# A new order for a two-layer hybrid encoder: differential pairs moved ahead, eps adds and scan copies on other engines, and a table that shifts the planner's priorities

## The chip, the cores and the metric

The kernel runs on one core of one Trainium2 chip. The metric is the device time of one execution in microseconds (us): before the change 1492.83 us, the median of three runs (1492.78 to 1493.38).

## The reference

Two layers on 512 tokens of width 1024, all in float32. Each layer projects the residual stream once into three groups of heads, joins their outputs in one output projection with a LayerNorm behind it, and then runs a gated MLP with a small convolution and another LayerNorm. Cut to what matters:

```python
proj = x @ w_in                                  # 1024 -> 4608
da_q, da_k, da_v, hg_q, hg_ff, hg_fb, hg_i, hg_g, mx_q = split(proj)
# differential attention, 4 heads: two softmaxes over 512 keys each
p = softmax(s); a = p[:, :, 0] - lam * p[:, :, 1]; da_o = rms_norm(a @ v)
# HGRN2: a gated linear recurrence, forward and backward, 4 heads with a 128x128 state
hg_o = rms_norm(scan(q, k, v, g) + flip(scan(flipped))) * silu(hg_g)
# cross-attention into 256 memory rows, 4 heads
mx_o = softmax(mx_q @ mk.T) @ mv
x = layer_norm(alpha * x + concat(da_o, hg_o, mx_o) @ w_out)
u = depthwise_conv(x @ w_up); gate, val = split(u)
x = layer_norm(alpha * x + (silu(gate) * val) @ w_down)
```

## The kernel before

**Numbers.** Every large product is done with float16 matmuls: weights and activations are each split into a high and a low part (`wh`, `wl`; `xh`, `xl`; `mgh`, `mgl`), and three products of the parts are summed in PSUM (`mm3`, L314; all large matmuls are issued by the helper at L140). A weight is prepared in these steps (`prep`, L295 to L312): SP loads it (`wst`), ScalarE squares it and sums (L307), a tiny matmul with ones adds the sums up over the partitions (`stat`, L168), VectorE makes a power of two from it (L155, L157, L159), ScalarE writes the scaled high part (L310) and VectorE the low part (L311). Activations are split in the same way by `split_group` (L531): ScalarE squares each half (L536), VectorE adds the halves' sums where there are two halves (L540), a tiny matmul and three small steps give the scale, and VectorE writes the high part (L545) and the low part (L547).

**The work.** The heads go in pairs: two pairs each of HGRN2 ("hg"), memory attention ("mx") and differential attention ("da"). A pair has projection steps on TensorE and a *unit*, which is a generator of small pieces of work. In an hg unit the scan runs over five small block lengths (1 to 16) and then larger ones; per length, VectorE masks the block of scores (L851) and multiplies decays into queries and keys (L881, L885), and at length 16 GpSimd copies the diagonal blocks (L854). In a da unit VectorE takes maxima (L1039, L1040), ScalarE the exponentials (L1042), VectorE combines the two softmaxes (L1049 to L1051), and TensorE transposes the result (L513). In an mx unit VectorE takes the maxima (L952), ScalarE the exponentials (L957), VectorE divides (L962, L964), TensorE transposes (L968), and the result is copied out (L975). The root of the mean square is in `rms` (L516), the LayerNorm in `norm` (L223) and `layernorm` (L274): statistics and first product on VectorE (L227, L229, L280), epsilon and the power -0.5 on GpSimd (L231, L232), the second product on VectorE (L281), transposes on TensorE (L288), and the split into `xh` and `xl` (L292, L293).

The output projection (`down_part`, L554) goes token tile by token tile: TensorE fills one PSUM bank (`mm`), and VectorE drains it into the residual tile `z` (L569). The next product into that bank waits for the drain. The pieces of the output projection are: hg pair 0, hg pair 1, da pair 0 (each of them a `down`), then four tiles of mx (`out_mx`), and at the end the rest of mx with da pair 1, with LayerNorm 1 token tile by token tile (`out_last`, L1104 ff.).

**What sets the order.** `SEQ` (L43) lists in which order pairs, the rotary set-up and output pieces are put beside each other; `emit` (L596) walks through it and lets the units' pieces run beside projection and output steps. That gives the program one order of writing. `extract` (L1285) then reads the program's instructions with their dependences, `deadlines` (L1573) gives each one a due time, counted back from its consumers with planned costs, and `simulate` (L1417) lists the work of every engine and the choice of buffers by these due times. The resulting order per engine is imposed on the program; each engine then works in this order and waits where an operand or a buffer isn't ready.

Of the kernel before, what the change touches and what calls it, by code (L numbers as in the profile page):

```python
# [15 lines left out]
AF = mybir.ActivationFunctionType  # L16
ALU = mybir.AluOpType
AX = mybir.AxisListType

P = 128  # L20
S = 512
D = 1024
# [19 lines left out]
START = "c0123wv"  # L42
_seq = [("hg", 0), ("rope",), ("hg", 1), ("mx", 0), ("mx", 1), ("da", 0), ("out", "hg", 0), ("da", 1), ("out", "hg", 1), ("out", "da", 0)]  # L43
SEQ = [_seq, _seq]
# [51 lines left out]
def trunk(ctx: ExitStack, tc: tile.TileContext, a, out, slots=None):  # L96
# [126 lines left out]
    def norm(t, idx):  # L223
        zt = z[t]
        st = small(12, "bnst")
        for j in range(2):
            V.bn_stats(st[:, j * 6 : (j + 1) * 6], zt[:, j * 512 : (j + 1) * 512])  # L227
        mv = small(2, "bnmv")
        V.bn_aggr(mv, st)  # L229
        rs = small(1, "lnrs")  # L230
        G.tensor_scalar(rs, mv[:, 1:2], LN_EPS / (ALPHA * ALPHA if idx else 1.0), None, ALU.add)  # L231
        G.tensor_tensor(rs, rs, mhalf[:, 0:1], ALU.pow)  # L232
        return mv[:, 0:1], rs
# [282 lines left out]
    def rms(o, eps=None):  # L516
        sq = tmp([P, 4, P], "w2", bufs=4)
        A.activation(sq, o.rearrange("p (c v) -> p c v", c=4), AF.Square)
        ss = small(4, "rmss")
        V.tensor_reduce(ss, sq, AX.X, ALU.add)  # L520
        rs = small(4, "rmrs")
        if eps is None:
            G.tensor_scalar(rs, ss, 1.0 / P, RMS_EPS, ALU.mult, ALU.add)
        else:
            G.tensor_tensor(rs, ss, eps, ALU.add)
        G.tensor_tensor(rs, rs, mhalf, ALU.pow)
        on = tmp([P, 4, P], "w2", bufs=4)
        V.tensor_tensor(on, o.rearrange("p (c v) -> p c v", c=4), rs.unsqueeze(2).broadcast_to([P, 4, P]), ALU.mult)
        return transposes(on)
# [162 lines left out]
    def build_layer(l):  # L692
# [55 lines left out]
        def hg_units(pr):  # L748
# [57 lines left out]
            def hg_attn():  # L806
# [31 lines left out]
                while m < S:  # L838
                    nb = S // m
                    for j in range(2):  # L840
                        Q, K, At, Dg, Tm = Qs[j], Ks[j], As[j], Ds[j], Ts[j]
                        p_ = psc()
                        if m <= 16:
# [8 lines left out]
                            if m == 16:  # L852
                                for b in range(4):
                                    G.tensor_copy(diag_block(At, 32 * b, 32 * b, 32), Dg[32 * b : 32 * b + 32])  # L854
                        elif m <= 64:
# [368 lines left out]
class Op:  # L1224
    __slots__ = ("i", "name", "eng", "cost", "tail", "reads", "writes", "table", "preds", "succs", "tiles", "dmab", "line", "kind", "small", "order_ins", "mv", "istr", "half", "mode")

# [58 lines left out]
def extract(instrs):  # L1285
    ops = []
    last_half = None
    for i in instrs:
# [28 lines left out]
        o.writes = [b for b in outs if type(b.tensor).__name__ == "Tile"]  # L1317
        o.preds, o.succs = set(), []
        o.small = _n(outs[0].ap) <= 16 if outs else False
# [44 lines left out]
    for o in ops:  # L1364
        o.tiles = []
        for wr, bs in ((False, o.reads), (True, o.writes)):
            for b in bs:
# [9 lines left out]
                for (j, w2, a0, a1, m2) in h:  # L1377
                    if (wr or w2) and j != o.i:
                        if psum or (a0 < p1 and p0 < a1 and m & m2):
                            o.preds.add(j)  # L1380
        for wr, bs in ((False, o.reads), (True, o.writes)):
            for b in bs:
# [3 lines left out]
                if wr:  # L1386
                    if psum:
                        h[:] = []
                    else:
                        h[:] = [e for e in h if not (p0 <= e[2] and e[3] <= p1 and (e[4] & ~m) == 0 and e[0] != o.i)]  # L1390
                h.append((o.i, wr, p0, p1, m))
    for o in [o for o in ops if o.dmab][:FIRST]:
        o.dmab *= FAST
# [23 lines left out]
def simulate(ops, tiles, prio, fixed=None, wait=0.0, log=None):  # L1417
# [8 lines left out]
    mode = 128  # L1426
    dma_free = 0.0

# [55 lines left out]
    while done < N:  # L1484
# [60 lines left out]
        for s in o.succs:  # L1545
            lat = LAT if ops[s].eng != o.eng else (0.03 if e != "PE" else -o.tail)
            if ops[s].eng == "POOL" and e != "POOL":
# [16 lines left out]


PEN = 20.0
SHARE = 0.35
# [5 lines left out]
def deadlines(ops, tiles):  # L1573
# [32 lines left out]
    for k, o in enumerate([o for o in ops if o.dmab][:FIRST]):  # L1606
        D[o.i] = k - 1000.0
    return [T[o.i] if o.eng == "PE" else D[o.i] for o in ops]

# [50 lines left out]
```

## Time and profile before

| what | value |
|---|---|
| runs | 1493.38, 1492.83, 1492.78 us; median 1492.83 |
| profiled execution | 1492.88 us, of which the span of the trace is 1491.1 us |
| TensorE (PE) busy | 1451.7 us, 97% |
| VectorE (DVE) busy | 1168.4 us, 78% |
| ScalarE (ACT) busy | 865.1 us, 58% |
| GpSimd (POOL) busy | 130.1 us, 9% |

How to read the profile: L12 is line 12 of the kernel before. A row of a view names engine, line, operation, and what it writes from what it reads, in the program's names without buffer numbers. "Busy" leaves out the issuing of DMAs and the work on semaphores. Matmuls are pipelined, so one that is drawn 0.38 us long may have its successor start after about 0.22. A time in brackets is the idle time of the engine just before a row, with the instruction that ended it. PEclk is the clock that TensorE was granted, as a share of full speed. In time, the span holds: the start to 21 us, projections and scans of layer 0 to about 300, output projection to about 430 with LayerNorm 1, the MLP to 800, scans of layer 1 to 960, its softmax groups and output projection to 1150, its MLP to 1482, and the tail.

### The profile page before, as it was taken

The page shows a single profiled execution, that of the slowest core. Times are in us where ns is not written, and L with a number is a line of the kernel's source. Part 1 is how long each engine was busy: PE and PEld are TensorE (multiplying, and loading weights), DVE is VectorE, ACT ScalarE, POOL GpSimd, SP SyncE. Part 2 cuts the span into 40 slices and gives each one's busy share as a digit, 9 for nine tenths or more (in the row PEclk, how much of TensorE's full clock was granted, in tenths as well). Part 3 has the DMA queues.
Part 4 walks back from the last instruction along what each step waited for, and adds up shares of the span by engine and source line. Part 5 has one row for each costly group of instructions (what it writes and reads, how often), then busy time and mean ns, then how long its engine had stood idle before and what let it go on. Part 6 is the DMA issues. An engine that isn't in the chain of part 4 may idle for free. (4 is left out here: it accounts for less than half of the span.)

```text
span 1491.1 us, 24496 instructions
## 1 busy us (share of the span) xinstructions
PE 1451.7 (97%) x9978; PEld 811.9 (54%) x9978; DVE 1168.4 (78%) x2242; ACT 865.1 (58%) x1094; POOL 130.1 (9%) x154
## 2 busy tenths in 40 slices
PE   6999999999999999999999999999999999999997
PEld 4566675565564444444487475655656544444443
DVE  7989968978997677666785978789888777566777
ACT  5876655666376556455466656566645656455550
POOL 1001020000111101001000101001001101001011
PEclk9999999999999999999999999999999999999999
DMA  6342111223143323232324202112232323333221
GB/s 238 114 150 86 59 58 59 101 71 101 46 143 114 107 85 113 85 113 96 128 90 140 87 30 86 57 57 77 79 100 85 113 88 118 99 92 114 86 84 57
DMA packets 158171, 141.91 MB, mean 95 GB/s; under 512 B 3302, under 2 KB 139114, under 8 KB 158058
## 3 DMA queue, kind: packets, MB, share of 16 engines
q1 hardware_dynamic: 158058, 140.35, 29.2%
q8 instruction: 78, 1.28, 0.3%
q14 instruction: 35, 0.29, 0.1%
HBM read 138.24 MB, written 2.10 MB: 94 GB/s over the span
## 5 line engine op out<-in xcount | busy, mean ns | idle before, releaser
L140 PEld LDWEIGHTS <-wh 128*128 128x128 f16 x2624 | 251.0, 98 | 237.5 <-issue 3.4
L311 DVE SCALAR_TENSOR_TENSOR wl<-wst,ws,wh 128x2048 f16<-128x2048 f32 x122 | 312.5, 2561 | 52.3 <-ACT wh L310 51.4
L140 PE MATMUL mm<-xh,wl 128*128 128x512 f16 (+1 forms) x832 | 305.3, 367 | 0.6 <-DVE wl L311 0.6
L140 PE MATMUL mm<-xh,wh 128*128 128x512 f16 (+1 forms) x832 | 305.2, 367 | 0.0
L140 PE MATMUL mm<-xl,wh 128*128 128x512 f16 (+1 forms) x832 | 305.0, 367 | 0.0
L307 ACT ACTIVATE wh<-wst 128x2048 bf16<-128x2048 f32 x122 | 232.2, 1903 | 102.4 <-PE stat L168 49.2
L310 ACT ACTIVATE wh<-wst,ws 128x2048 f16<-128x2048 f32 x122 | 243.5, 1996 | 40.1 <-DVE ws L157 19.5
L140 PE MATMUL mm<-wh,t 128*128 128x512 f16 (+1 forms) x768 | 223.5, 370 | 0.0
L140 PEld LDWEIGHTS <-wl 128*128 128x128 f16 x1312 | 128.2, 98 | 123.0 <-DVE wl L311 0.9
L140 PEld LDWEIGHTS <-t 128*128 128x128 f16 x1152 | 110.2, 98 | 121.4 <-issue 0.6
L569 DVE SCALAR_TENSOR_TENSOR z<-mm,inv,z 128x512 f32<-128x512 f32 x176 | 130.2, 745 | 45.9 <-PE mm L140 32.2
L140 PE MATMUL sc<-xl,wh 128*128 128x512 f16 (+1 forms) x416 | 147.5, 355 | 0.0
L140 PE MATMUL sc<-xh,wl 128*128 128x512 f16 (+1 forms) x416 | 147.5, 355 | 0.0
L140 PE MATMUL sc<-xh,wh 128*128 128x512 f16 (+1 forms) x416 | 147.5, 355 | 0.0
L140 PE MATMUL mm<-wl,t 128*128 128x512 f16 (+1 forms) x384 | 142.1, 370 | 0.0
L155 DVE TENSOR_SCALAR we<-stat 128x1 int32<-128x1 int32 x122 | 18.6, 153 | 118.8 <-PE stat L168 118.6
L1151 POOL TENSOR_TENSOR t<-f 128x512 f32<-128x512 f32 x44 | 60.6, 1378 | 542.7 <-DVE f L1149 438.6
L140 PE MATMUL mm<-wh,mgh 128*128 128x512 f16 x192 | 73.3, 382 | 4.7 <-DVE z L569 4.7
L1147 ACT ACTIVATE f<-sc,cvb,cw 128x512 f32<-128x512 f32 x44 | 34.1, 775 | 71.4 <-PE stat L168 69.3
L140 PE MATMUL mm<-wh,mgl 128*128 128x512 f16 x192 | 72.9, 381 | 0.9 <-DVE mgl L547 0.6
L140 PE MATMUL mm<-wl,mgh 128*128 128x512 f16 x192 | 73.3, 382 | 0.0
L1042 ACT ACTIVATE f<-sc,dam,iqk 128x512 f32<-128x512 f32 x64 | 49.3, 774 | 38.8 <-DVE dam L1040 34.3
(244 smaller groups left out, 2125.4 us busy)
## 6 DMA issues: line engine op xcount, KB each, us to landing
wst<-in_w_up_dram SPq DMA_DIRECT2D x88, 512.0 KB, 4.3
wst<-in_w_in_dram SPq DMA_DIRECT2D x36, 1024.0 KB, 4.8
wst<-in_w_down_dram SPq DMA_DIRECT2D x22, 1024.0 KB, 4.9
wst<-in_w_out_dram SPq DMA_DIRECT2D x12, 1024.0 KB, 4.9
wst<-in_w_mem_kv_dram SPq DMA_DIRECT2D x8, 1024.0 KB, 5.0
z<-in_x_dram SPq DMA_DIRECT2D x4, 512.0 KB, 4.9
mix<-in_ln_g_dram SPq DMA_DIRECT2D x4, 512.0 KB, 3.6
mix<-in_ln_b_dram SPq DMA_DIRECT2D x4, 512.0 KB, 4.7
```

Of the source, the lines that this page charges most:

```text
L140: T.matmul(o, lhsT, rhs, start=start, stop=stop)
L155: V.tensor_scalar(e, tot.bitcast(I32), 0x7F000000, 1, ALU.bitwise_and, ALU.logical_shift_right)
L307: A.activation(h.rearrange("p a b -> p (a b)").bitcast(BF16), flat, AF.Square, accum_out=ss)
L310: A.activation(h.rearrange("p a b -> p (a b)"), flat, AF.Identity, scale=s)
L311: V.scalar_tensor_tensor(l.rearrange("p a b -> p (a b)"), flat, s, h.rearrange("p a b -> p (a b)"), ALU.mult, ALU.subtract)
L569: V.scalar_tensor_tensor(zs, p_, ivs[half % len(ivs)], zs, ALU.mult, ALU.add)
L1042: A.activation(pe[:, c, :], sc_[c], AF.Exp, bias=mx[:, c : c + 1], scale=iqk, accum_out=z1 if c else z0)
L1147: A.activation(c, p_, AF.Identity, scale=cw[:, 1, v : v + 1], bias=cvb[:, l, i + 22 * v : i + 22 * v + 1])
L1151: G.tensor_tensor(gt[:, n, :], c2[:, 0, :], c2[:, 1, :], ALU.mult)
```

## The change

1. `SEQ` is rewritten: the da pairs come right behind the hg pairs and the mx pairs behind them; of the output pieces, hg pair 0, hg pair 1 and da pair 0 now stand at the end. (Before, the mx pairs came first, and the output pieces stood between and behind the da pairs.)
2. The epsilon adds of `norm` and `rms` (L231, L523, L525) go from GpSimd to VectorE; the power -0.5 stays on GpSimd.
3. The copies of the diagonal blocks at length 16 (L854, 32 of 32x128) go from GpSimd to ScalarE.
4. The planner: an order between two reads of the same PSUM bank by one engine is kept in its planning as "soft" with a latency of its own, the first DMA is planned 2.1 us later, and a table `NUDGE` of some 280 rows (engine, from, to, shift) adds shifts to the due times of ranges of instructions.

```diff
-_seq = [("hg", 0), ("rope",), ("hg", 1), ("mx", 0), ("mx", 1), ("da", 0), ("out", "hg", 0), ("da", 1), ("out", "hg", 1), ("out", "da", 0)]
+_seq = [("hg", 0), ("rope",), ("hg", 1), ("da", 0), ("da", 1), ("mx", 0), ("mx", 1), ("out", "hg", 0), ("out", "hg", 1), ("out", "da", 0)]
...
-        G.tensor_scalar(rs, mv[:, 1:2], LN_EPS / (ALPHA * ALPHA if idx else 1.0), None, ALU.add)
+        V.tensor_scalar(rs, mv[:, 1:2], LN_EPS / (ALPHA * ALPHA if idx else 1.0), None, ALU.add)
...
-            G.tensor_scalar(rs, ss, 1.0 / P, RMS_EPS, ALU.mult, ALU.add)
+            V.tensor_scalar(rs, ss, 1.0 / P, RMS_EPS, ALU.mult, ALU.add)
         else:
-            G.tensor_tensor(rs, ss, eps, ALU.add)
+            V.tensor_tensor(rs, ss, eps, ALU.add)
...
-                                    G.tensor_copy(diag_block(At, 32 * b, 32 * b, 32), Dg[32 * b : 32 * b + 32])
+                                    A.activation(diag_block(At, 32 * b, 32 * b, 32), Dg[32 * b : 32 * b + 32], AF.Identity)
...
+                    elif psum and j != o.i and ops[j].eng == o.eng:
+                        o.soft.add(j)
...
+    for o in ops:
+        o.soft -= o.preds
+        o.preds |= o.soft
...
-    dma_free = 0.0
+    dma_free = 2.1
...
-            lat = LAT if ops[s].eng != o.eng else (0.03 if e != "PE" else -o.tail)
+            lat = LAT if ops[s].eng != o.eng else (0.03 if e != "PE" and i not in ops[s].soft else -o.tail)
...
+    (0, 2171, 2215, -9.43), (2, 8523, 8601, 7.46), (1, 3505, 3534, -45.27), (2, 8524, 8545, 0.73), (1, 7, 17, -1.14), (1, 9160, 9161, 8.8),
...
-    return [T[o.i] if o.eng == "PE" else D[o.i] for o in ops]
+    D = [T[o.i] if o.eng == "PE" else D[o.i] for o in ops]
+    for e, a, b, d in NUDGE:
+        for o in ops[a:b]:
+            if o.eng == ("PE", "DVE", "ACT", "POOL", "SP")[e]:
+                D[o.i] += d
+    return D
```

The first place is the queue of VectorE inside the softmax run of the differential pairs in layer 0, before the change (`f4` are softmax tiles, `dam` maxima, `daz1` sums, `z0` to `z3` the residual token tiles, `mm` a PSUM bank of the output projection):

```order
L569 SCALAR_TENSOR_TENSOR z1_78<-mm_740_4152,inv_726_4092,z1_78 128x512
L1049 RECIPROCAL daz1_679_3884<-daz1_679_3884 128x1
L1050 SCALAR_TENSOR_TENSOR daz1_679_3884<-daz1_679_3884,nlam0_328,daz_673_3867 128x1
L1039 TENSOR_REDUCE dam_687_3911<-sc_689_3913 128x1
L1039 TENSOR_REDUCE dam_687_3911<-sc_690_3914 128x1
L1051 SCALAR_TENSOR_TENSOR f4_681_3886<-f4_681_3886,daz1_679_3884 128x512
L1040 TENSOR_SCALAR dam_687_3911<-dam_687_3911,iqk_661_3796 128x2
L569 SCALAR_TENSOR_TENSOR z2_79<-mm_747_4185,inv_726_4092,z2_79 128x512
L311 SCALAR_TENSOR_TENSOR wl_725_4089<-wst_719_4077,ws_723_4085,wh_720_4079 128x2048
L569 SCALAR_TENSOR_TENSOR z3_80<-mm_749_4202,inv_726_4092,z3_80 128x512
```

The same kind of work in VectorE's queue after the change:

```order
L1040 TENSOR_SCALAR dam_578_3427<-dam_578_3427,iqk_559_3338 128x2
L1051 SCALAR_TENSOR_TENSOR f4_574_3412<-f4_574_3412,daz1_572_3410 128x512
L311 SCALAR_TENSOR_TENSOR wl_623_3631<-wst_617_3619,ws_621_3627,wh_618_3621 128x2048
L1049 RECIPROCAL daz1_577_3426<-daz1_577_3426 128x1
L1050 SCALAR_TENSOR_TENSOR daz1_577_3426<-daz1_577_3426,nlam0_328,daz_571_3409 128x1
L1039 TENSOR_REDUCE dam_585_3453<-sc_587_3455 128x1
L1039 TENSOR_REDUCE dam_585_3453<-sc_588_3456 128x1
L1051 SCALAR_TENSOR_TENSOR f4_579_3428<-f4_579_3428,daz1_577_3426 128x512
```

The drains (L569) that stood between the softmax steps are gone from this run; weights (L311) stand there as before. Between the first and the last L1051 of a layer there were 23 and 22 drains, and now there are 3 and 0. In the runs of the mx units (L952 to L975) there were none, and now there are 21 and 14.

The second place is the split of the mx halves in layer 1, on VectorE. Before, around the sum of the halves (`gss1`):

```order
L1040 TENSOR_SCALAR dam_1818_10627<-dam_1818_10627,iqk_1778_10411 128x2
L569 SCALAR_TENSOR_TENSOR z3_80<-mm_1879_10891,inv_1837_10692,z3_80 128x512
L540 TENSOR_REDUCE gss1_1757_10312<-gss_1754_10307 128x1
L157 TENSOR_SCALAR ws_1884_10907<-we_1883_10905 128x1
L159 TENSOR_SCALAR wi_1885_10909<-we_1883_10905 128x1
L326 TENSOR_SCALAR inv_1916_11082<-wi_1885_10909,lnin_82 128x1
L155 TENSOR_SCALAR ge_1759_10316<-tr_1758_10314 128x1
L157 TENSOR_SCALAR gs_1760_10318<-ge_1759_10316 128x1
L159 TENSOR_SCALAR gi_1761_10320<-ge_1759_10316 128x1
L545 TENSOR_SCALAR mgh_1755_10308<-mix_1676_9961,gs_1760_10318 128x1024
```

After the change (`mm_2025` is the bank of the last output product of da pair 0):

```order
L569 SCALAR_TENSOR_TENSOR z3_80<-mm_2025_11626,inv_2017_11568,z3_80 128x512
L326 TENSOR_SCALAR inv_2062_11761<-wi_2031_11644,gi_1903_11084 128x1
L540 TENSOR_REDUCE gss1_1984_11432<-gss_1981_11427 128x1
L155 TENSOR_SCALAR ge_1986_11436<-tr_1985_11434 128x1
L157 TENSOR_SCALAR gs_1987_11438<-ge_1986_11436 128x1
L159 TENSOR_SCALAR gi_1988_11440<-ge_1986_11436 128x1
L545 TENSOR_SCALAR mgh_1982_11428<-mix_1916_11136,gs_1987_11438 128x1024
L326 TENSOR_SCALAR inv_2040_11665<-wi_1999_11482,gi_1988_11440 128x1
L547 SCALAR_TENSOR_TENSOR mgl_1989_11443<-mix_1916_11136,gs_1987_11438,mgh_1982_11428 128x1024
```

And TensorE's rows at that place after the change:

```order
L140 MATMUL mm_2025_11626<-wl_1949_11279,mgh_1786_10511 128x512
L140 LDWEIGHTS mgl_1791_10522
L140 MATMUL mm_2025_11626<-wh_1944_11269,mgl_1791_10522 128x512
L168 LDWEIGHTS ones_74
L168 MATMUL tr_1985_11434<-gss1_1984_11432,ones_74 128x1
L140 LDWEIGHTS mgh_1982_11428
L140 MATMUL mm_2042_11669<-wh_1995_11474,mgh_1982_11428 128x512
```

The split moved from the middle of the softmax work to the last moment: its sum stands behind the drain of the product that TensorE finishes just ahead of the split's own tiny matmul. In layer 0 the order is the same.

The third place is VectorE at LayerNorm 1 of layer 1, before the change (`z1_78` and `z2_79` are the second and third token tile):

```order
L229 BN_AGGR bnmv_2073_11824<-bnst_2072_11821 128x2
L192 TENSOR_SCALAR lnbd_2058_11750<-lnbd_2058_11750 128x1
L280 SCALAR_TENSOR_TENSOR z1_78<-z1_78,bnmv_2073_11824,mix_2054_11742 128x512
L155 TENSOR_SCALAR lne_2059_11753<-lnbd_2058_11750 128x1
L280 SCALAR_TENSOR_TENSOR z1_78<-z1_78,bnmv_2073_11824,mix_2054_11742 128x512
L157 TENSOR_SCALAR lns_2060_11755<-lne_2059_11753 128x1
L281 SCALAR_TENSOR_TENSOR z1_78<-z1_78,lnrs_2074_11826,mix_2056_11746 128x512
L194 COPY lnsc_81<-lns_2060_11755 128x1
L281 SCALAR_TENSOR_TENSOR z1_78<-z1_78,lnrs_2074_11826,mix_2056_11746 128x512
L569 SCALAR_TENSOR_TENSOR z2_79<-mm_2077_11847,inv_2040_11665,z2_79 128x512
```

And after it:

```order
L229 BN_AGGR bnmv_2066_11782<-bnst_2065_11779 128x2
L227 BN_STATS bnst_2072_11821<-z1_78 128x6
L231 TENSOR_SCALAR lnrs_2067_11784<-bnmv_2066_11782 128x1
L280 SCALAR_TENSOR_TENSOR z0_77<-z0_77,bnmv_2066_11782,mix_2054_11742 128x512 x2
L281 SCALAR_TENSOR_TENSOR z0_77<-z0_77,lnrs_2067_11784,mix_2056_11746 128x512 x2
L569 SCALAR_TENSOR_TENSOR z2_79<-mm_2077_11847,inv_2040_11665,z2_79 128x512
L229 BN_AGGR bnmv_2073_11824<-bnst_2072_11821 128x2
L231 TENSOR_SCALAR lnrs_2074_11826<-bnmv_2073_11824 128x1
```

The same drain (from `mm_2077`) stood behind the second tile's whole normalization and now stands ahead of it, and the epsilon add (L231) is among VectorE's rows.

More of the change, by code (lines that the diff above doesn't have):

```diff
@@ L1224 @@
 class Op:
-    __slots__ = ("i", "name", "eng", "cost", "tail", "reads", "writes", "table", "preds", "succs", "tiles", "dmab", "line", "kind", "small", "order_ins", "mv", "istr", "half", "mode")
+    __slots__ = ("i", "name", "eng", "cost", "tail", "reads", "writes", "table", "preds", "succs", "tiles", "dmab", "line", "kind", "small", "order_ins", "mv", "istr", "half", "mode", "soft")
 def cost_of(i, kind, eng, outs, ins):
@@ L1317, in extract @@
         o.writes = [b for b in outs if type(b.tensor).__name__ == "Tile"]
-        o.preds, o.succs = set(), []
+        o.preds, o.succs, o.soft = set(), [], set()
         o.small = _n(outs[0].ap) <= 16 if outs else False
@@ L1563, in simulate @@
     return max(end), start, end, order, slot_of
+NUDGE = (
[44 rows of a table added]
+)
 PEN = 20.0
```

43 rows, old and new, of the table NUDGE are left out of this document.

## The prediction

> **What bounds the kernel now.** I read the page's busy shares first, then the table of stretches, then the waits of TensorE stretch by stretch, then the timeline around the longest wait. A busy share first:
>
> ```profile
> PE 1451.7 (97%) x9978; PEld 811.9 (54%) x9978; DVE 1168.4 (78%) x2242; ACT 865.1 (58%) x1094; POOL 130.1 (9%) x154
> ```
>
> TensorE (PE) is the bound: 97% of the span of 1491.1 us. The change adds no matmul, so it can only win where PE stands idle or runs slowly. The table of stretches says where that is (columns: stretch, its length, then busy time and count for PE, weight loads, VectorE, ScalarE, POOL; then granted clock):
>
> ```profile
> core 0: us, PE busy (x) PEld busy (x) DVE busy (x) ACT busy (x) POOL busy (x), PEclk, DMA share, GB/s
> 0.00:21.00 21.00, 6.23 (x25) 4.06 (x26) 13.96 (x41) 9.49 (x10) 3.83 (x14) 1.00 0.82 304
> 75.00:300.00 225.00, 222.69 (x2242) 138.70 (x2241) 194.81 (x446) 146.84 (x228) 17.77 (x25) 1.00 0.26 85
> 300.00:400.00 100.00, 95.80 (x587) 55.89 (x585) 83.59 (x170) 53.29 (x84) 8.31 (x12) 1.00 0.25 80
> 800.00:960.00 160.00, 156.84 (x1801) 98.59 (x1800) 128.70 (x290) 96.27 (x145) 16.19 (x24) 1.00 0.20 67
> 960.00:1110.00 150.00, 147.77 (x925) 87.16 (x923) 130.69 (x275) 94.46 (x158) 6.69 (x8) 1.00 0.25 80
> 1110.00:1150.00 40.00, 37.18 (x233) 23.77 (x232) 36.44 (x70) 16.08 (x18) 5.99 (x8) 0.96 0.22 72
> ```
>
> Length less PE busy is idle time: 14.8 us at the start, 2.3 and 3.2 in the two scans (75 to 300 and 800 to 960), 4.2 and 2.2 in the two stretches with differential attention and output projection (300 to 400, 960 to 1110), 2.8 around the first LayerNorm of layer 1, the only stretch of these whose clock is below 1.00. The waits of PE say for whom it stood (total us, times, longest); first 300 to 400, then 960 to 1110, then the scans:
>
> ```profile
> PE tr L513 <- DVE f L1051: 2.1, 2, 1.3
> ```
>
> ```profile
> PE mm L140 <- DVE z L569: 1.4, 3, 0.8
> ```
>
> ```profile
> PE sc L140 <- DVE hgD L851: 0.8, 2, 0.4
> ```
>
> ```profile
> PE sc L140 <- DVE t L881: 1.2, 3, 0.5
> PE sc L140 <- DVE hgD L851: 1.2, 3, 0.4
> ```
>
> All are waits for VectorE (DVE): for the combination of the two softmaxes (L1051), for a drain of the output projection (L569), for masked scan blocks (L851) and decay products (L881). The longest of all is in the fourth place, the timeline at 1118 to 1127 (start, length, engine, operation, and in brackets the idle time ahead of it and who ended that):
>
> ```profile
> 1118.43 0.60 PE L288 MATMUL tr<-cst,z 128*128 128x128 f32 x4
> 1118.87 0.38 PE L140 MATMUL mm<-wh,mgl 128*128 128x512 f16 x1
> 1119.09 0.38 PE L140 MATMUL mm<-wh,mgh 128*128 128x512 f16 x1
> 1119.12 0.78 POOL L231 TENSOR_SCALAR lnrs<-bnmv 128x1 f32<-128x1 f32 x1 [3.88 <-DVE lnbd L192]
> ...
> 1119.98 1.00 POOL L232 TENSOR_TENSOR lnrs<-lnrs,mhalf 128x1 f32<-128x1 f32 x1
> ...
> 1121.01 0.75 DVE L281 SCALAR_TENSOR_TENSOR z<-z,lnrs,mix 128x512 f32<-128x512 f32 x1 [0.41 <-POOL lnrs L232]
> ...
> 1122.40 0.74 DVE L569 SCALAR_TENSOR_TENSOR z<-mm,inv,z 128x512 f32<-128x512 f32 x1
> ...
> 1123.20 0.58 PE L140 MATMUL mm<-wh,mgh 128*128 128x512 f16 x1 [2.66 <-DVE z L569]
> ...
> 1123.58 0.63 PE L140 MATMUL mm<-wl,mgh 128*128 128x512 f16 x1
> ...
> 1126.82 0.38 PE L140 MATMUL mm<-wh,mgl 128*128 128x512 f16 x1
> ```
>
> PE needs the PSUM bank that the drain at 1122.40 empties. That drain is queued on DVE behind the normalization of an earlier token tile, and this one waits for POOL. PE stands 2.66 us; after that its matmuls last 0.63 instead of 0.38 until 1126.82. Between 1123.20 and 1126.82 lie 5 matmuls and 8 transposes. At full rate a matmul takes 0.22 (1118.87 to 1119.09) and four transposes 0.44 (1118.43 to 1118.87), so that work needs 2.0 and takes 3.6: the wait costs another 1.6 in clock, 4.3 in all. A shown gap elsewhere costs about 0.16 more than the view says, since the last matmul before it is drawn 0.38 long where the next could follow after 0.22.
>
> **The change part by part.** The sum is made against the profiled execution, 1492.88 us, 0.05 above the median.
>
> *LayerNorm 1 of layer 1.* In the new order the drain that PE waits for stands directly behind the first tile's two L281; the second tile's block (two L280, the POOL wait, two L281: from 1119.07 to 1122.40, over 3 us of DVE queue) now comes after it. PE stopped at 1123.20 - 2.66 = 1120.54, and the drain can then start before that. Bounds: 0 (another drain takes its place) to -4.3. I take **-4.1**, since the cover moved is longer than the gap.
>
> *Differential attention beside projections.* With both pairs right behind the scan pairs, their softmax runs lie beside input projections, which have no L569. In the order of DVE, the drains between first and last L1051 of a layer's run go from 23 and 22 to 3 and 0: 42 of 45. The idle time there is 4.2 + 2.2 = 6.4, and with 13 gaps at 0.16 some 8.5 us. By the share of drains, 42/45, that is **-7.9**.
>
> *Memory attention beside the output projection.* This is the same thing backwards: between first and last step of the memory-attention runs (L952 to L975) there stood no drain, now 21 and 14. At the price that the 45 had, 8.5/45 = 0.19 each, that is +6.6; the other bound is 0, because a memory head has a quarter of the scores of a differential one and its chain of small steps is shorter. I take a third, nearer to 0 since DVE has no second softmax to combine there: **+2.2**.
>
> *The split of the memory halves.* Before, this split lay among projection steps. Now PE's rows are: last output matmul of differential pair 0, the tiny stat product for the split, then at once the matmuls with the split's result. On DVE the sum that the stat needs (L540) stands behind the drain of that same last matmul. So nothing covers the chain. Its pieces, from the groups by tile (min/median/max in ns):
>
> ```profile
> L569 DVE SCALAR_TENSOR_TENSOR z<-mm,inv,z x176: 701/746/752, 266.1 to 1481.8; 128x512 f32<-128x512 f32 x176
> ```
>
> ```profile
> L540 DVE TENSOR_REDUCE gss<-gss x2: 144/144/145, 280.9 to 1013.3; 128x1 f32<-128x2 f32 x2
> ```
>
> ```profile
> L155 DVE TENSOR_SCALAR ge<-tr x22: 130/158/159, 154.6 to 1447.3; 128x1 int32<-128x1 int32 x22
> ```
>
> ```profile
> L545 DVE TENSOR_SCALAR mgh<-mix,gs x12: 744/751/754, 155.1 to 1106.8; 128x1024 f16<-128x1024 f32 x12
> L547 DVE SCALAR_TENSOR_TENSOR mgl<-mix,gs,mgh x12: 1268/1280/1286, 156.2 to 1108.1; 128x1024 f16<-128x1024 f32 x12
> ```
>
> Drain 0.75, one small step 0.16, sum 0.14: PE waits 1.05 for the stat. Then three small steps of 0.16 and L545: 1.2, with hand-overs 1.3. Then PE has four matmuls (0.9) while L547 and a small step take 1.45: 0.55. The second half's L545 and L547 (2.0 and a small step) against nine matmuls (2.0): 0.25. Together 3.2 a layer, **+6.4**. The clock: in the row above one gap of 2.66 cost 1.6. Here 2.4 lie in two gaps with only a stat between; I put half of it at each layer, **+1.6** (bounds 0 and 3.2).
>
> The Trainium skill, "TensorE: Matmul & The Clock Gate", section "Why this matters for your kernels", says that a matmul stream loses its clock only through idle gaps over about 3 us. The trace differs: the gap of 2.66 already came with matmuls of 0.63, and the measurement decides. By that rule the slow matmuls would not hang on the gap, the first term would be -2.5, the clock part here nil, and the sum the same.
>
> *Scan copies on ScalarE.* Their rows, on POOL now, and the same shape on ScalarE:
>
> ```profile
> L854 POOL COPY t<-hgD x32: 279/392/3775, 114.7 to 919.7; 32x128 f32<-32x128 f32 x32
> ```
>
> ```profile
> L862 ACT ACTIVATE t<-sc x48: 249/269/379, 115.0 to 921.5; 32x128 f32<-32x128 f32 x32, 64x256 f32<-64x256 f32 x16
> ```
>
> 32 x 0.27 = 8.6 us come to ScalarE, whose idle time in the first scan alone is 225 - 147 = 78 us; that covers it, and without the cover it would be the 8.6. The consumers get their blocks no later. What PE waits for in the scans are L851 and L881 on DVE: 3.2 of the 5.5 us idle. The change gives DVE no less work there, only another order. Bounds: -7.4 (all idle and 12 gaps at 0.16) to +2 (four more gaps of the longest shown, 0.5); I take **-0.9**, a small part, because the waiting steps and their engine stay.
>
> *The start.* On ScalarE the two L264 for the first token columns now stand ahead of the second weight's L307:
>
> ```profile
> 14.80 1.91 ACT L307 ACTIVATE wh<-wst 128x2048 bf16<-128x2048 f32 x1 [0.72 <-DMA wst<-in_w_in_dram]
> ...
> 15.06 0.69 PE L262 MATMUL tr<-cst,z 128*128 128x128 f32 x2 [0.20 <-DVE z L258]
> ...
> 16.71 1.43 ACT L264 ACTIVATE w<-tr,gbc 128x512 f32<-128x512 f32 x2
> ...
> 18.03 1.99 ACT L310 ACTIVATE wh<-wst,ws 128x2048 f16<-128x2048 f32 x1
> ...
> 20.07 0.37 PE L140 MATMUL mm<-wh,xh 128*128 128x256 f16 x1 [0.59 <-ACT wh L310]
> ...
> 35.54 0.38 PE L140 MATMUL mm<-xh,wh 128*128 128x512 f16 x1
> ```
>
> The transposes that L264 reads end at 15.75, so it can start about 0.8 sooner, and L310 and the first matmul with it: **-0.7** (0 to -0.8). The second weight comes later, but the first product with it is the one at 35.54, 15.5 us after the first matmul, so its L307, L310 and L311 (some 6 us in all) are hidden; without that cover they would be the price.
>
> *The tail.* The epsilon add goes from POOL (0.78, row 1119.12) to DVE (one column, 0.16):
>
> ```profile
> 1484.67 1.41 DVE L280 SCALAR_TENSOR_TENSOR z<-z,bnmv,mix 128x512 f32<-128x512 f32 x2
> ...
> 1486.54 1.41 DVE L281 SCALAR_TENSOR_TENSOR z<-z,lnrs,mix 128x512 f32<-128x512 f32 x2 [0.46 <-POOL lnrs L232]
> ```
>
> DVE's last wait for POOL, 0.46, goes; the add costs 0.16: **-0.3**. Elsewhere these adds are some 0.2 each on a DVE that is idle a fifth of the time.
>
> *Groups of half-height matmuls.* Each switch to 64-row work costs PE about 0.09 (the next matmul could begin at 272.75):
>
> ```profile
> 272.53 0.38 PE L140 MATMUL mm<-wl,mgh 128*128 128x512 f16 x1
> ...
> 272.84 0.82 PE L140 MATMUL sc<-qg,qg 64*128 64x512 f16 x6
> ```
>
> The order has 65 such groups instead of 69; at 0.09 to 0.19 with the way back, **-0.6**.
>
> Sum: -4.1 - 7.9 + 2.2 + 6.4 + 1.6 - 0.9 - 0.7 - 0.3 - 0.6 = -4.3, so 1488.6.
>
> **The rivals.** *The covers hold* (0.25): memory attention takes the drains at no cost, the scans win half of their bound (-3.7), the splits keep the clock. Then -4.1 - 7.9 + 6.4 - 3.7 - 1.6 = -10.9: 1482. For it: no wait of PE for a memory step is among the rows of before. Against it: then no drain stood there.
>
> *The stalls only move* (0.17): memory attention pays the drains' full price (+6.6) and both splits lose the clock (+3.2): 1488.6 + 4.4 + 1.6 = 1494.6, no change. By the skill's rule on gaps above, the last 1.6 could not come.
>
> *Slower: the memory runs pay double* (0.13). Each memory unit hands over twice between PE and DVE (scores to maximum, quotient L964 to transposes), and a drain can stand in both. At 0.38 a drain the term is +13.3, and the time 1488.6 + 11.1 = 1499.7. It decides from 0.27 a drain: 35 x 0.27 = 9.4 is 7.2 over the 2.2 taken, and 1488.6 + 7.2 is the 1495.8 from which I call it slower. For it: DVE is the engine that PE waits for. Against it: it is idle a fifth of the time there too.
>
> That the change does not do what it says is excluded by the order, which shows every move named here.
>
> **How the numbers follow.** The forecast has 0.45, its own range 1485 to 1491.5. A difference of 0.2% is what a measurement of this kernel can tell from none: faster is below 1489.85, slower above 1495.8. Faster: three quarters of the forecast's 0.45 and the 0.25 of the covers, 0.59. Slower: 0.13 and a little of the moved stalls, 0.16. The same: 0.25. The range for 8 in 10 leaves out the far half of the covers' case and most of the slower one: 1479 to 1496.5.
>
> **What would show it.** In the profile after: no wait of PE for L569 over 1 us at the first LayerNorm of layer 1, and its clock at 1.00; hardly any wait for L1051; in each layer a pair of waits over 1 us, for L540 and for L545, behind the output projection of differential pair 0; the first matmul at about 19.4. I am wrong if the waits at the splits are missing, if transposes of memory attention (L968) wait for L964 by more than 3 us in all, or if the scans' waits for L851 and L881 change by more than 3 us.

## The result and the profile after

The changed kernel takes 1481.3 us (median of 4 runs, 1480.8 to 1481.86) against 1492.8 us before: ratio 0.9922, 95% interval 0.9905 to 0.994, 11.5 us faster. The profiled execution took 1480.8 us, its span 1479.0, 12.1 less than before. A later set of runs of the same kernel (e10) gave 1480.53 us (ratio 0.992, 0.9907 to 0.9934).

The page and the table of stretches after, with the columns of before:

```profile
PE 1447.6 (98%) x9978; PEld 809.7 (55%) x9978; DVE 1161.1 (79%) x2278; ACT 867.8 (59%) x1124; POOL 97.7 (7%) x86
```

```profile
0.00:21.00 21.00, 7.68 (x32) 5.42 (x33) 15.11 (x42) 9.21 (x9) 3.92 (x10) 1.00 0.82 304
75.00:300.00 225.00, 222.79 (x2300) 140.59 (x2298) 198.77 (x452) 154.15 (x240) 6.74 (x6) 1.00 0.26 86
300.00:400.00 100.00, 97.37 (x527) 54.15 (x528) 84.99 (x182) 52.06 (x93) 4.99 (x5) 0.98 0.24 77
800.00:960.00 160.00, 159.27 (x1854) 100.57 (x1851) 139.55 (x310) 101.93 (x157) 4.78 (x4) 1.00 0.24 79
960.00:1110.00 150.00, 146.54 (x871) 83.43 (x868) 125.64 (x279) 90.91 (x162) 6.54 (x5) 0.99 0.22 73
1110.00:1150.00 40.00, 40.00 (x300) 29.31 (x299) 36.38 (x66) 22.12 (x24) 3.10 (x4) 1.00 0.33 102
```

TensorE's idle time is 2.2 us in the first scan (2.3 before), 0.7 in the second (3.2), 2.6 from 300 to 400 (4.2), 3.5 from 960 to 1110 (2.2, so more), and nothing around the LayerNorm of layer 1 (2.8), where the clock is back at 1.00. The stretches are the same times of the span as before, so the work in them has moved by some us: the differential runs now lie at the end of the scan stretches. The clock is now low in the two stretches that had it full before. The waits of TensorE over the whole span, without those of the start:

```profile
PE mm L140 <- DVE mgh L545: 2.5, 2, 1.2
PE tr L168 <- DVE gss L540: 2.4, 2, 1.2
...
PE sc L140 <- DVE hgD L851: 0.9, 2, 0.5
...
PE tr L513 <- DVE f L1051: 0.5, 2, 0.3
PE mm L140 <- DVE z L569: 0.4, 1, 0.4
```

The two largest are the two halves of the memory split, one pair in each layer. All else is small: L569 had 4.7 in 6 waits before, L881 1.5 in 4, and no wait for L881 is left. The split of layer 0 on TensorE:

```profile
363.43 0.38 PE L140 MATMUL mm<-wh,mgl 128*128 128x512 f16 x1
365.02 0.18 PE L168 MATMUL tr<-gss,ones 128*128 128x1 bf16 x1 [1.22 <-DVE gss L540]
366.43 0.61 PE L140 MATMUL mm<-wh,mgh 128*128 128x512 f16 x1 [1.23 <-DVE mgh L545]
366.82 0.63 PE L140 MATMUL mm<-wl,mgh 128*128 128x512 f16 x1
...
369.38 0.38 PE L140 MATMUL mm<-wh,mgl 128*128 128x512 f16 x1
```

Two gaps of 1.2, then 7 matmuls that take 2.95 us (366.43 to 369.38) where 1.5 would do. Layer 1 shows the same (1.21 and 1.23, then 8 slow matmuls). The start, all engines:

```profile
15.08 1.45 ACT L264 ACTIVATE w<-tr,gbc 128x512 f32<-128x512 f32 x2 [1.01 <-PE tr L262]
...
16.41 2.00 ACT L310 ACTIVATE wh<-wst,ws 128x2048 f16<-128x2048 f32 x1
...
18.46 0.37 PE L140 MATMUL mm<-wh,xh 128*128 128x256 f16 x1 [0.59 <-ACT wh L310]
```

```profile
21.42 0.27 PE L140 MATMUL sc<-wh,xl 128*128 128x256 f16 x1
...
32.81 0.38 PE L140 MATMUL mm<-xh,wh 128*128 128x512 f16 x1
```

The first matmul comes 1.6 us sooner than before (20.07), the first 512-wide one 2.7 sooner (35.54).

### The profile page after: what moved, and what is told of

It is laid out like the page before. It is cut to its first block, busy times and chain, and to the rows that moved or that the text cites. A ratio compares the mean times of both kernels' runs of the same rounds, so it can differ in the third digit from the quotient of the medians.

```text
span 1479.0 us, 24485 instructions
## 1 busy us (share of the span) xinstructions
PE 1447.6 (98%) x9978; PEld 809.7 (55%) x9978; DVE 1161.1 (79%) x2278; ACT 867.8 (59%) x1124; POOL 97.7 (7%) x86
## 4 chain that ended last, share of the span: by engine, by line
PE 92%; DVE 5%; ACT 1%; issue 1%; POOL 0%; DMA 0%; SPq 0%; DVEq 0%; ACTq 0%; POOLq 0%
PE mm L140 63%; PE sc L140 21%; PE tr L140 5%; PE tr L513 1%; DVE t L881 1%; DVE wl L311 1%; PE tr L288 1%; DVE t L885 1%; PE tr L968 1%; DVE bnst L227 0%; ACT wh L310 0%; DVE z L569 0%; ACT wh L307 0%; PE tr L379 0%; DMA z<-in_x_dram 0%
## 5 line engine op out<-in xcount | busy, mean ns | idle before, releaser
L311 DVE SCALAR_TENSOR_TENSOR wl<-wst,ws,wh 128x2048 f16<-128x2048 f32 x122 | 304.5, 2497 | 47.2 <-ACT wh L310 46.7
L307 ACT ACTIVATE wh<-wst 128x2048 bf16<-128x2048 f32 x122 | 232.3, 1904 | 100.4 <-PE mm L140 39.8
L310 ACT ACTIVATE wh<-wst,ws 128x2048 f16<-128x2048 f32 x122 | 243.5, 1997 | 59.1 <-DVE wi L159 41.7
L569 DVE SCALAR_TENSOR_TENSOR z<-mm,inv,z 128x512 f32<-128x512 f32 x176 | 130.6, 746 | 56.4 <-PE mm L140 50.2
L140 PE MATMUL mm<-wh,xh 128*128 128x256 f16 x240 | 64.1, 274 | 0.6 <-ACT wh L310 0.6
L140 PE MATMUL mm<-wh,xl 128*128 128x256 f16 x240 | 64.3, 274 | 0.0
```

The source lines that it names most:

```text
L140: T.matmul(o, lhsT, rhs, start=start, stop=stop)
L307: A.activation(h.rearrange("p a b -> p (a b)").bitcast(BF16), flat, AF.Square, accum_out=ss)
L310: A.activation(h.rearrange("p a b -> p (a b)"), flat, AF.Identity, scale=s)
L311: V.scalar_tensor_tensor(l.rearrange("p a b -> p (a b)"), flat, s, h.rearrange("p a b -> p (a b)"), ALU.mult, ALU.subtract)
L569: V.scalar_tensor_tensor(zs, p_, ivs[half % len(ivs)], zs, ALU.mult, ALU.add)
```

## The experiments

The theory at this point: the gain is the sum of small waits that the new order takes away, in the LayerNorm of layer 1, the softmax runs, the scans and the start, less 8.6 us for two splits without cover. The rivals: the new sequence alone carries it; the engine moves carry it; the table carries it; the splits cost nothing that could be had.

**e1, cover for the split.** In `out_last` the first token tile of differential pair 1 goes ahead of the memory tiles, of which `out_mx` no longer writes any; the table is unchanged:

```diff
             for t in range(TT):
-                while ol["n"] < 2 * t + 2:
-                    ...
                 for half in range(2):
                     da(half, t)
                     yield
+                while ol["n"] < max(MX_EARLY, 2 * t + 2):
+                    ...
```

> The changed kernel, but the first token tile of differential pair 1's output product is issued ahead of the memory product, so that TensorE has 12 matmuls (2.6 us) while the memory halves are split. Theory: the two splits cost 4.2 us a layer (two gaps of 1.2 and 7 slow matmuls after them); with this cover the clock dip goes in both layers and one gap of the two, so about 2.8 a layer: 1475 to 1477. Rival: the memory chain itself ends too late, and the wait only moves behind the new matmuls: 1480 to 1482.

Measured: 1490.23 us, ratio 0.9981 (0.9971 to 0.999). Neither. The new writing order shifts due times backward through the program, and the table, whose rows are instruction numbers of another program, no longer fits: new waits turned up, most of them in layer 1, where TensorE stands idle 8.3 us from 960 to 1110 (3.5 in the changed kernel) and the weight of the cover came late (waits of 1.5 and 1.3 for L310 and L307). In layer 0 the cover kept the clock (1.00 from 300 to 400) in this trace. So this run doesn't tell what a cover is worth in time. That the table is at fault is borne out by e8 below, the same program with a table of its own, 7.5 us faster.

**e2, e3, e4: the sequence alone, the engine moves alone, everything but the table.** e2 is the kernel before with the new `SEQ` line; e3 is the kernel before with the four lines of the diff that change engines; e4 is the changed kernel with

```diff
-NUDGE = (
-    ...
-)
+NUDGE = ()
```

> The kernel before with the new SEQ alone, planned anew without the table, the engine moves or the soft order. Theory: the new sequence takes the drains out of the differential runs (about -6 net of the memory runs) and pays 8.4 for the uncovered split, so it is 1491 to 1497 by itself. Rival: the sequence carries the gain, 1481 to 1485, and the table only trims.

> The kernel before with the epsilon adds on VectorE and the scan copies on ScalarE, planned anew. Theory: only the tail (0.3) and little in the LayerNorm of layer 1 hang on GpSimd by themselves: 1490 to 1493. Rival: GpSimd's share of the waits is what the change removes, the 2.66 us wait of layer 1 goes with it: 1486 to 1488.

> The changed kernel with an empty table, planned anew: new sequence, engine moves and soft order are all in. Theory: most of the gain sits in places that the table shifts one by one (the start, the LayerNorm of layer 1, the scans), so 1488 to 1494. Rival: sequence and engines carry it, 1481 to 1485.

Measured: e2 1497.13 us, ratio 1.0035 (1.0022 to 1.0048), slower; e3 1493.14, ratio 1.0007 (0.9998 to 1.0017); e4 1492.98, ratio 1.0001 (0.9992 to 1.001). e4 lies in the theory's range, e2 and e3 0.1 us above its upper end; the rivals' ranges are missed by 5 to 12 us. The ten executions of e3 fall into two groups, 1491.66 to 1492.21 us with a mean granted clock of 0.998 or 0.999 and 1494.06 to 1496.16 with 0.995 or 0.996, so its median lies between two values and not at one; neither group comes near its rival. Without the table the whole change is worth nothing; with it, 11.5 us. TensorE's waits in e2:

```profile
PE mm L140 <- DVE z L569: 3.6, 4, 1.4
...
PE tr L168 <- DVE gss L540: 3.1, 2, 1.9
PE mm L140 <- DVE mgh L545: 2.8, 2, 1.5
PE sc L140 <- DVE hgD L851: 2.4, 6, 0.7
...
PE sc L140 <- DVE t L881: 1.2, 3, 0.5
```

The wait for L1051 is gone here (it stands in none of the rows), and so are all drains from the differential runs. But the splits have come (5.9 in all), L569 still costs 3.6, and the scans have 3.6 in these two rows. In e4's second scan alone TensorE waits for L851 (1.1), L727 (0.8), L885 (0.7) and L881 (0.5); in the changed kernel that stretch has 0.7 in all. What the table does is to take such waits away one by one.

**e5, e6: the adds or the copies back on GpSimd, in the same order.** The plan is made for the changed kernel, and then only these instructions are moved into GpSimd's queue, at the place where the plan had them:

```diff
-        V.tensor_scalar(rs, mv[:, 1:2], LN_EPS / ...)
+        (G if FIXED[0] else V).tensor_scalar(rs, mv[:, 1:2], LN_EPS / ...)
```

```diff
-    A.activation(diag_block(At, 32 * b, 32 * b, 32), Dg[...], AF.Identity)
+    if FIXED[0]:
+        G.tensor_copy(diag_block(At, 32 * b, 32 * b, 32), Dg[...])
```

> The changed kernel with its order kept row for row, but the epsilon adds back on GpSimd (moved from VectorE's queue into GpSimd's, ahead of their powers). Theory: the adds stood in the chain of the first normalization, and the start owes them most of its 2.7 us (first 512-wide matmul at 32.8 instead of 35.5), with 0.3 in the tail: 1483 to 1485. Rival: the start owes its gain to the order of ScalarE, and only the tail hangs on the adds: 1481 to 1482.

> The changed kernel with its order kept, but the 32 scan copies back on GpSimd. Theory: TensorE waits in the scans for VectorE, not for the copies, so nothing changes: 1480.5 to 1482. Rival: a copy on GpSimd (up to 3.8 us in the trace of before) holds up its scan, and the change gained there: 1483 to 1487.

Measured: e5 1481.69 us, ratio 0.9926 (0.9912 to 0.9941); e6 1481.07, ratio 0.992 (0.9906 to 0.9935). For e5 the rival holds: the start owes most of its gain to the order. Its first matmul and the tail:

```profile
18.93 0.37 PE L140 MATMUL mm<-wh,xh 128*128 128x256 f16 x1 [0.59 <-ACT wh L310]
```

```profile
1473.56 1.42 DVE L280 SCALAR_TENSOR_TENSOR z<-z,bnmv,mix 128x512 f32<-128x512 f32 x2
1475.43 1.42 DVE L281 SCALAR_TENSOR_TENSOR z<-z,lnrs,mix 128x512 f32<-128x512 f32 x2 [0.46 <-POOL lnrs L232]
```

The first matmul is 0.5 later than with the adds on VectorE (18.46) and still 1.1 earlier than before; the tail has its wait of 0.46 again. Other orders have an early first matmul too: it starts at 18.68 in e3 (old sequence, no table) and at 18.61 in e9 below (old sequence, adds on GpSimd, a table of its own), so neither the new sequence nor the adds on VectorE are needed for it. The copies back on GpSimd change nothing, as the theory had it.

**e7, TensorE kept busy through the splits.** The order is the changed kernel's; 11 products of ones with ones, whose results nobody reads, are put on either side of the tiny matmul of each memory split:

```diff
+        for k in range(KEEP if busy else 0):
+            T.matmul(bank[:, 256:384], ones, ones, start=True, stop=True)
         T.matmul(tot, ones, ss.bitcast(BF16)[:, 1:2], start=True, stop=True)
         r = pow2_of(tot, n, tag)
+        for k in range(KEEP if busy else 0):
+            T.matmul(bank[:, 256:384], ones, ones, start=True, stop=True)
```

> The changed kernel with its order kept, and 11 small matmuls of ones with ones ahead of the tiny matmul of each split of the memory halves and 11 behind it, their results unused, so that TensorE is busy through the two gaps of 1.2 us. Theory: the 7 matmuls at 0.63 us behind each split come from the idle time; with it filled they run at 0.38 and each layer saves 1.4: 1478 to 1479.5. Rival: they are slow for another reason, or the fill delays the split: 1481 to 1483.

Measured: 1480.39 us, ratio 0.9916 (0.99 to 0.9933), between the two expectations and not to be told from the changed kernel by its time. The trace tells more: behind both splits all matmuls last 0.38 or 0.39. From the last matmul ahead of the split to the weight's stat product behind it, layer 0 took 6.17 us (363.43 to 369.60) and takes 5.18 (364.26 to 369.44). The saving is 1.0 a layer instead of 1.4, because at full rate TensorE reaches the low part (L547) 0.3 us too early and waits for it.

**e8, e9: two programs with tables of their own.** e8 is the program of e1 and e9 the kernel before (old sequence, adds and copies on GpSimd) with the new planning; each has a table that was found by local search for it.

> The program of e1_cover (first tile of differential pair 1's output product ahead of the memory product), but with a table of its own, found by the same kind of local search for this program. Theory: with the order trimmed as well as in the changed kernel, the cover shows: the wait for L540 goes, four matmuls stand against the 2.0 us from L540 to the end of L545, about 1.0 idle is left in each layer and the clock holds, so 6 of the 8.6 us of both splits are saved: 1473 to 1477. Rival: the splits' cost is bound to the late end of the memory chain and comes back there: 1480 to 1483.

> The kernel before with its old sequence, the epsilon adds and copies on GpSimd as before, but with the soft order in the planning and a table of its own, found by local search for this program. Theory: the table is what pays, on any sequence, since the new sequence and the engines alone bring nothing: 1480 to 1486. Rival: the new sequence is what makes room for a table: 1489 to 1493.

> The changed kernel once more, on the chip of the two others: 1481 to 1482 by every theory.

Measured on one chip: e8 1482.77 us, ratio 0.9937 (0.9925 to 0.995); e9 1484.35, ratio 0.9947 (0.9933 to 0.996); e10 1480.53, ratio 0.992. For e9 the theory holds: a table with the new planning, on the old sequence and the old engines, brings 8.2 of the 12.0 us that the whole change brings on that chip. (The new planning without a table was not run on the old sequence; in e4, where it is in, the whole is worth nothing.) And it does so with 22 drains in each layer's differential run, where before there were 23 and 22; its trace has no wait of TensorE for L1051 at all.

For e8 the theory fails in the sum and holds in part at the place; the time is in the rival's range. The stretches with the scans and the splits in them:

```profile
75.00:300.00 225.00, 220.68 (x2292) 140.16 (x2290) 197.22 (x454) 155.99 (x239) 6.94 (x6) 1.00 0.26 85
300.00:400.00 100.00, 98.25 (x533) 53.80 (x534) 87.46 (x187) 52.46 (x93) 6.10 (x5) 1.00 0.25 80
...
800.00:960.00 160.00, 157.44 (x1840) 100.82 (x1839) 134.17 (x301) 99.17 (x149) 5.24 (x4) 1.00 0.22 74
960.00:1110.00 150.00, 148.22 (x887) 84.84 (x886) 129.23 (x279) 96.86 (x173) 5.03 (x5) 0.99 0.24 78
```

The idle time falls from 2.6 to 1.75 and from 3.5 to 1.8 us in the second and fourth row, and layer 0 keeps its clock (1.00). No wait for L540 is left at the splits, as forecast. But part of the cost comes back behind the cover, as the rival had it: TensorE now waits for the low part (L547), 0.7 us in layer 0 and 1.25 in layer 1. With the smaller waits ahead of these, the gaps of both splits are still 2.8 us against 4.9, and layer 1 loses its clock (0.99 in the fourth row). And the scans stand idle 4.3 and 2.6 us, against 2.2 and 0.7 in the changed kernel: this table is worse there. A kernel with this cover and scans as well ordered as the changed kernel's was not made, so how much of the 8.6 can be had stays open.

**e11, e12: only one of the two gaps filled.** e7 with one of its two loops left out.

> The changed kernel, its order kept, with the 11 unused matmuls only ahead of the split's tiny matmul: the second gap of 1.2 us stays. Theory: single gaps up to 1.6 us are followed by matmuls of 0.38 in every trace so far, and only idle time that adds up (two gaps of 1.2 with a tiny matmul between) costs the clock; so all matmuls behind the split run at 0.38: 1479 to 1480.5. Rival: the gap right ahead of the matmuls costs the clock by itself: 0.63 as before, 1481 to 1482.

> The same with the 11 unused matmuls only behind the tiny matmul: the first gap of 1.2 us stays. Theory of adding up: 0.38 as well, 1479 to 1480.5. Rival: the clock follows the first gap with a delay, and the matmuls run at 0.63 as before: 1481 to 1482.

Measured: e11 1480.29 us, ratio 0.9913 (0.9896 to 0.9929); e12 1479.92, ratio 0.9913 (0.9898 to 0.9928). The split of layer 0, e11:

```profile
365.57 0.16 PE L172 MATMUL tr<-gss,ones 128*128 128x1 bf16 x1 [0.60 <-DVE gss L547]
366.97 0.51 PE L140 MATMUL mm<-wh,mgh 128*128 128x512 f16 x1 [1.23 <-DVE mgh L552]
367.27 0.63 PE L140 MATMUL mm<-wl,mgh 128*128 128x512 f16 x1
```

And e12:

```profile
364.65 0.18 PE L172 MATMUL tr<-gss,ones 128*128 128x1 bf16 x1 [1.22 <-DVE gss L547]
365.08 0.77 PE L175 MATMUL tr<-ones 128*128 128x128 bf16 x11 [0.25 <-DVE ge L155]
366.06 0.39 PE L140 MATMUL mm<-wh,mgh 128*128 128x512 f16 x1 [0.21 <-DVE mgh L552]
366.29 0.38 PE L140 MATMUL mm<-wl,mgh 128*128 128x512 f16 x1
```

In the trace of e11, with the first gap filled, the clock is lost as before, in both layers; in that of e12, with the second filled, it holds, in both layers. So in these two traces my theory was right for e12 and wrong for e11. But a trace is one execution, and executions of one kernel differ. The mean granted clock of e11's four was 0.995 (the traced one, 1481.57 us), 0.998 (1479.15), 0.997 (1480.49) and 0.997 (1480.08); of e12's, 0.999 (the traced one, 1479.36), 0.997 (1480.79), 0.998 (1479.34) and 0.997 (1480.48). The changed kernel itself had 0.996 twice (1481.16 and 1481.53) and 0.998 twice (1479.90 and 1479.62) in e10, and e7 had 0.998 in all four. That filling the second gap keeps the clock and filling the first does not is therefore not shown; the last section says what decides it in the traces. e12 has the lowest median of all kernels here, 1.4 us under the changed kernel's first set and 0.6 under its second; the intervals overlap, so that it beats the changed kernel is not shown.

## Why the prediction was right or wrong

The time lies inside the range (1479 to 1496.5) and on the likelier side; the forecast's own 1488.6 is 7.3 us too high and its own range (1485 to 1491.5) missed. Of the rivals, *the covers hold* (1482) came closest in time, but not by its mechanism: it had the splits keep their clock, and in the trace they lost it. Point by point, forecast first:

| term | forecast | measured | by what |
|---|---|---|---|
| LayerNorm 1 of layer 1 | -4.1 | about -4.7 | idle 2.8 before, none after; 1.6 of slow matmuls gone; 0.16 for each of 2 gaps |
| differential and memory runs | -5.7 | about -6.8 | idle 6.4 before, 1.2 after outside the splits, and 0.16 for each of 10 gaps fewer |
| half-height groups | -0.6 | about -2.3 | see below |
| memory split | +8.0 | +8.6 | gaps 4.9, drawn ends 0.6, slow matmuls 1.4 and 1.65 |
| scans | -0.9 | about -3.0 | idle 5.5 before, 2.9 after, and an estimated 0.5 for fewer gaps |
| start | -0.7 | -2.7 | first 512-wide matmul, 35.54 and 32.81 |
| tail | -0.3 | -0.3 | last matmul's end to the end of the span: 9.28 and 8.97 |

These are -11.2 of -12.1 us. The rows go by one trace of each kernel and by stretches whose work has moved, so they are rough; where the rest lies was not followed.

**Right, with its mechanism:** the drain in front of the LayerNorm, the tail, and the memory split, whose place, two waits, their lengths (1.05 and 1.3 forecast, 1.22 and 1.23 measured) and clock loss came out of the order and the durations alone. Its later pieces were wrong in detail: the waits for the low parts (0.8 a layer in my sum) did not come, because TensorE was slow by then; both layers lost the clock in the trace, which cost 3.05 where I had put 1.6; and I had left out the drawn ends of the four gaps (0.6). These errors cancel, so that 8.0 came so near to 8.6 is in part luck. The first wait had another end in layer 0, too: behind the drain the sum L540 still waited 0.21 us for ScalarE's square (L536).

**Mis-sized: the start.** I gave it the 0.7 that the two L264 win on ScalarE. The transposes themselves also came sooner (the eight at 17.52 before stand at 15.91), through the order of VectorE's first normalizations and, by e5, 0.5 from the adds; and the sooner start brought the full clock sooner. TensorE runs its first matmuls at half rate, to about 23.9 before:

```profile
23.66 0.42 PE L140 MATMUL sc<-wh,xh 128*128 128x256 f16 x1
23.87 0.40 PE L140 MATMUL mm<-wh,xh 128*128 128x256 f16 x1
24.08 0.29 PE L140 MATMUL sc<-wh,xh 128*128 128x256 f16 x1
```

After, they are at 0.27 by 21.42. So the full rate comes 2.7 us sooner where the first matmul comes 1.6 sooner. Part of this is chance of the two executions. With the order of the changed kernel's start, the full rate came between 19.9 us (e12) and 22.7 (e7), and the first 512-wide matmul between 32.35 (e6) and 33.60 (e7); with the old start it came at 34.87 in e2. By these traces the start is worth between 1.3 and 3.2 us.

**Mis-sized: the scans.** The step that failed reads "The change gives DVE no less work there, only another order", from which I took a small part of the bound. Order was enough: the second scan's idle time went from 3.2 to 0.7 us, with no less work on VectorE in that stretch (128.7 us busy before, 139.6 after). I had said it would prove me wrong if these waits changed by more than 3 us; those for L851 and L881 fell by 2.5 (3.4 to 0.9), just below.

**Right in size, wrong in its reason: the differential runs.** I priced the drains that leave them, 0.19 each, and charged a third of that to the memory runs. Where the drains left the run (e2, e4) the wait for L1051 left too, as I had it. But e9 has 22 drains in each run and no wait for L1051 either, and its idle time from 300 to 400 and from 960 to 1110 is 3.1 us, where before it was 6.4. So a drain in the run has no fixed price. Whether it delays a softmax seems to depend on where in the run it stands, and that is what a table can move; which shifts do it was not traced. No wait for a step of the memory runs came (L964 stands in none of the rows after), so what the rivals charged there (*the stalls only move*, *the memory runs pay double*) did not come either.

**What I did not see at all** is how the gain divides among the parts of the change. I read the final order and priced its places, which was right as a method, since the order is what runs; but the text speaks as if the sequence made it ("With both pairs right behind the scan pairs"). By e2 to e4 and e9 the sequence and the engine moves are worth +4.4 and about 0 by themselves, and the table is worth 11.7 on the new program (e4 to the change), and 8.2 on the old one together with the new planning.

**The half-height groups** hold a price I had left out. A group of six 64-row matmuls takes 0.75 us. The matmuls of a group start two at a time. In the trace of before, four of the 32 groups began with one matmul alone: without idle time this took 1.03 us (at 1083.21), and the other three took 1.5 to 1.8 us up to their successor, with 0.4 to 0.6 of idle time inside or right behind them. Four more were cut in two. After, one is cut, and all whole groups take 0.75 or 0.76. In all, the 192 matmuls took 27.9 us up to their successors and now 24.2, of which 1.4 is idle time counted above.

## What to carry to other kernels

Where one engine is busy 97% of the time, price a change of order by places: find each spot where the engine's next instruction hangs on a queue whose last entry it has only just fed, and add up durations. A sequence, an engine move and a table of shifts are not additive: a table belongs to one exact program, and after a change of the program (e1: 1490.23 us with the old table; e8: 1482.77 with its own) it has to be found again before anything can be concluded. And hold a planned order fixed when one operation's engine is on trial (e5, e6), or the accidents of a new plan, here up to 9 us (e1), hide the answer.

## What the runs showed of the hardware

Idle time costs TensorE its clock in a pattern that I had not expected. Two gaps of 1.2 us with one tiny matmul between them (2.45 idle in 2.6 us) were followed by 7 or 8 matmuls of 0.63 us in both layers of the changed kernel, and again in both layers of the traces of e5, e6 and e10 and in layer 0 of e4; in layer 1 of e4 four matmuls still went at full rate, and the slow ones came behind a third gap, of 0.8. Single gaps before matmuls of full width did not: in e4

```profile
358.38 0.38 PE L140 MATMUL mm<-wh,mgh 128*128 128x512 f16 x1 [1.17 <-DVE z L569]
358.60 0.38 PE L140 MATMUL mm<-wl,mgh 128*128 128x512 f16 x1
```

and in e2 after 1.35. Nor did 1.58 and 0.78 in e3, with four float32 transposes between them:

```profile
1123.77 0.63 PE L288 MATMUL tr<-cst,z 128*128 128x128 f32 x4 [1.58 <-DVE z L281]
1125.17 0.27 PE L140 MATMUL sc<-xh,wh 128*128 128x256 f16 x1 [0.78 <-ACT xh L292]
1125.28 0.62 PE L288 MATMUL tr<-cst,z 128*128 128x128 f32 x4
1125.74 0.38 PE L140 MATMUL mm<-wh,mgh 128*128 128x512 f16 x1
```

A sum of the idle time at a place doesn't sort these cases: e3's 2.36 us kept the clock, and e11's 1.83 lost it twice. A sum over the right stretch of time does. In every trace the granted clock changes only at points that lie a whole multiple of 3.413 us apart: in the changed kernel's trace it rises at 21.21, falls at 365.95 (101 times 3.413 later), rises at 369.37 and falls at 1089.58 (211 times). A fall lasts 3.41 us, and 6.83 in e1 and in layer 0 of e2. Cut into these stretches of 3.41 us, and up to the last matmul, the 14 traces have 17 stretches at full rate with half rate behind them, and each of these has 1.77 us of TensorE's idle time or more; every stretch at full rate with full rate behind it has 1.59 or less. Here are two neighbouring stretches of e3 and two of e8 (start and end, length, TensorE's busy time; the granted clock is the third number from the end):

```profile
1120.64:1124.05 3.41, 1.83 (x12) 0.88 (x11) 3.39 (x9) 1.26 (x2) 1.06 (x1) 1.00 0.00 0
1124.05:1127.47 3.42, 2.64 (x18) 1.45 (x16) 3.42 (x6) 1.38 (x2) 0.00 (x0) 1.00 0.00 0
```

```profile
1093.70:1097.11 3.41, 1.64 (x7) 0.42 (x6) 3.41 (x5) 0.46 (x2) 0.00 (x0) 1.00 0.01 2
1097.11:1100.52 3.41, 3.41 (x10) 1.17 (x9) 1.64 (x7) 1.93 (x2) 0.00 (x0) 0.50 0.80 240
```

In e3 the gaps of 1.58 and 0.78 lie in two stretches, and the clock holds. In e8 gaps of 0.30, 0.22 and 1.25 lie in one; three matmuls still run at full rate behind the last gap, and the clock falls at 1097.11, where TensorE isn't idle at all.

Where the points lie against the program differs from execution to execution: the first rise comes at 19.86 us in e12's trace and at 22.73 in e7's, with the same order of the start. So the same two gaps can fall into one stretch or be divided between two. That would explain why e10 has the changed kernel at 0.996 and at 0.998; only one execution of each run was traced, so this is inferred. The Trainium skill, "TensorE: Matmul & The Clock Gate", Part 1, puts the switch to half rate behind an idle window of about 3.4 us. The traces agree with the length and differ in the rest: away from the start no gap was longer than 2.66, and 1.77 us of idle time in a stretch of 3.41 were enough.

What helped in practice is e7: with both gaps filled by 11 small matmuls without use, the four gaps left come to 1.33 us in layer 0, below 1.59 wherever the points lie, and its mean clock was 0.998 in all four executions. With one gap filled, up to 1.83 us (e11) or 1.68 (e12) can fall into one stretch, and their clocks varied.
